# A two-layer decoder trunk: four gated heads kept on chip, two sets of transposes tied behind matmul passes, and another order at the end of the attention

## The chip, the cores and the metric

The kernel runs on one core of one Trainium2 chip. Its time is device microseconds of one execution; the figure compared is the median of several runs. Profiles are single executions taken by the hardware profiler. In them PE is TensorE's matmuls and PEld its weight loads, DVE is VectorE, ACT is ScalarE, POOL is GpSimd, and SP is the engine whose queue issues nearly all the DMAs here. Times in a trace count from the first instruction.

## The reference, cut to what matters

The model has two layers on a sequence of 512 tokens of width 1024, float32 throughout. Layer 0 mixes tokens with a gated delta rule of 16 heads, layer 1 with causal sliding-window attention, and each is followed by a gated MLP with a causal convolution of width 3:

```python
h = h + gated_deltanet(rmsnorm(h, a_norm_w[i]), ...)      # layer 0
k_sh, v_sh = shared_kv(h, kv_norm_w, w_kv)
h = h + sliding_window_sink_attention(rmsnorm(h, b_norm_w[j]), k_sh, v_sh, ...)  # layer 1
h = h + conv_gated_mlp(rmsnorm(h, ffn_norm_w[layer]), ...)  # after each mixer
```

Three steps of it are touched. The mixer ends with a gate and a projection: `o = rmsnorm(o, out_norm_w) * silu(z)`, then `o @ w_out`. The attention projects the normalised residual once to keys and values (`rmsnorm(h, kv_norm_w) @ w_kv`), and its own queries from `rmsnorm(h, b_norm_w)`. It ends with `o @ w_o`, where `o` gathers 16 heads' `probs @ v`, two heads to each of eight row blocks of 128.

## The kernel before, in words

Everything is kept transposed: channels on the 128 partitions, the 512 tokens along the free dimension, so that a *row* is a tile of 128 x 512. A float32 product is made of three matmuls: weights and activations are split into a high and a low part (`hi` rounded by a cast on ACT, `lo` the rest by a subtraction on DVE; `cast` for weights, `split` for rows), and `mm3` (L158) adds hi·hi (L162), hi·lo (L163) and lo·hi (L164) for each of the contraction blocks. A *pass* is eight blocks of three matmuls into one PSUM bank. The split weights stand in three pairs of buffers, `whi` and `wlo`; the PSUM banks are three of tag `d` (passes), two of `g` (transposes and small products), two of `s` and one of `p`.

**Who sets the order.** Each engine takes its instructions in order, and SP its DMAs. That order is not the program's: the framework's planner counts through the kernel with costs of its own and gives each engine, when it is free, the ready instruction of the highest priority. In the mixer the string `ORDER` lists jobs (one letter each: P, I, Q, V, C for the stages of the delta rule, z for a gate's projection, g for a gate), and `SHIFT` moves a letter's priority; g is moved forward by 40 places. `behind(later, earlier)` (L176) adds an order without a semaphore: the planner may not set `later` before `earlier`. Only the attention's main loop is written out by hand for TensorE (`manual_schedule`). Buffers of one tag are used in rotation: an instruction that fills a tile waits until all readers of that buffer's last tile are done.

**The columns.** Vectors that are needed as one value per partition (norm gains, convolution taps) are loaded as rows and turned by TensorE through a `g` bank into `const` tiles, in `columns` (L207, the transpose at L215, the copy out on DVE at L217). The last two calls turn the MLP's convolution taps, `fcw`. Near them in the program lie the gates' transposes, which are already tied behind the fifth block of query 0's pass (L350, tied at L759), the copy of the gates on ACT (L354), and the first products of keys (`key_norms`, L414), which also use `g`.

**The gated heads.** After the recurrence (`scan`, L607, four chunks for each of four groups of heads; its state row is `us`) the outputs lie in scratch memory in DRAM (`od`), as do the silu'd gates (`zd`, from `gate_proj`, L685). `gate(h)` (L692) loads both, scales the output's tokens on ACT (L700), turns it with four transposes on TensorE (L703), multiplies by gain and gate on DVE (L704) and stores the row to a third scratch, `yd` (L705). Heads 0 to 11 use the rows `ol` and `zl`, heads 12 to 15 `dt` (four buffers) and `va` (two buffers). The output projection then loads all 16 rows back from `yd` (L801), splits each into high and low, and runs the passes of `a_w_out`, three banks open at a time. Between them TensorE turns the input x into the residual (L821), also through `g`, with ACT copying out (L822).

**The attention** (L1140). A pass each for two key tiles and two value tiles; DVE scales them (L1158); keys are split by ACT and DVE (L1164 to L1167), values are turned by TensorE (L1171) and copied out by ACT (L1172) to `Vp`. Then `normed` makes the query's split activations, `xh` on ACT (L172) and `xl` on DVE (L173), and queries 0 and 1 follow, matmul by matmul (`one_by_one`: L1181, L1183, L1185). The loop over 16 units u then interleaves by hand: `scores(u)` (L1224, softmax on DVE and ACT up to L1253), `values(u - 2)` (L1276), `turn_back(u - 1)` (the transposes of the probabilities, L1260, copied to `pT` rows by ACT, L1262), and 12 or 11 matmuls from a stream of dense work, which holds queries 2 to 7 and the first five of eight contraction blocks of output tiles 0, 1 and 2. Behind the loop stand `values(14)`, the rest of the stream, `turn_back(15)`, blocks 5 and 6 of the three output tiles (18 matmuls), `values(15)`, and block 7 tile by tile, with each tile's addition to the residual (L1311) behind its last matmul. `values` of an odd unit ends a row block: ACT and DVE split it (L168, L169) into `ah` and `al`. Output tiles 3 to 7 follow under the planner.

Of the kernel before, what the change touches and what calls it, by code (L numbers as in the profile page):

```python
# [12 lines left out]
ALU = mybir.AluOpType  # L13
# [4 lines left out]
P = 128  # L18
# [3 lines left out]
KD = D // P  # L22
# [19 lines left out]
def kernel(  # L42
# [27 lines left out]
    V, S, G, PE, SP = nc.vector, nc.scalar, nc.gpsimd, nc.tensor, nc.sync  # L70
# [36 lines left out]
    def row(tag, dt=F32, n=T):  # L107
        return main.tile([P, n], dt, tag=tag, bufs=ROWS[tag], name=nm(tag))
# [67 lines left out]
    def behind(later, earlier):  # L176
        info = mybir.DependencyInfo(mybir.DependencyClass.NoSync, mybir.DependencyReason.DATA)
        tc.add_manual_dep(later.ins, earlier.ins.name, info, reason="order of issue")
# [8 lines left out]
    first = wpool.tile([P, 8, 256], F32, tag="stage", bufs=2, name=nm("stage"))  # L187
    for i in range(2):
        cs = slice(HQK * P + i * P, HQK * P + (i + 1) * P)
# [4 lines left out]
    ident = const([P, P], s="ident")  # L194
# [9 lines left out]
    S.activation(warm[:], epsc[:], AF.Sqrt)  # L204


    def columns(parts, n, s, q=SP, tag="acc"):  # L207
        st = row(tag, n=P)
        r = 0
        for ap in parts:  # L210
            k = ap.shape[0]
            q.dma_start(st[r : r + k, :], ap)
            r += k
        ps = bank("g")
        PE.transpose(ps[:, :n], st[:n, :], ident[:n, :n])  # L215
        t = const([P, n], s=s)
        V.tensor_copy(t[:], ps[:, :n])  # L217
        return t
# [23 lines left out]
    xh, xl = [], []  # L242
    for k in range(KD):
        ps = bank("g") if k % 2 else bank("s")
        for c in range(NC):
            PE.transpose(ps[:, c * P : (c + 1) * P], xs[c][:, k * P : (k + 1) * P], ident[:])
        h, l = row("xh", F32R), row("xl", F32R)
# [18 lines left out]
    st = [{} for _ in range(4)]  # L266
# [422 lines left out]
        SP.dma_start(zd[h], sz[:])  # L689


    def gate(h):  # L692
        ot, y = (row("ol"), row("zl")) if h < 12 else (row("dt"), row("va"))
        o3 = ot[:].rearrange("p (c e) -> p c e", c=NC)
        j = h % 4
        SP.dma_start(o3, od[h // 4, :, :, j * P : (j + 1) * P])
        SP.dma_start(y[:], zd[h])
        for c in range(NC):
            cs = slice(c * P, (c + 1) * P)
            S.activation(ot[:, cs], ot[:, cs], AF.Copy, scale=f_c[:, h, c : c + 1])  # L700
        pt = bank("g")
        for c in range(NC):
            PE.transpose(pt[:, c * P : (c + 1) * P], ot[:, c * P : (c + 1) * P], ident[:])  # L703
        V.scalar_tensor_tensor(y[:], pt[:], onw_c[:, 8:9], y[:], op0=ALU.mult, op1=ALU.mult)  # L704
        SP.dma_start(yd[h], y[:])  # L705

# [36 lines left out]
    for i, line in enumerate(ORDER):  # L745
        for word in line.split():
# [3 lines left out]
            with tc.high_priority(tc.cur_priority - target):  # L750
# [5 lines left out]
                else:  # L756
                    JOBS[a.upper()](i - 1, *n)

    for t in turned_gates:  # L759
        behind(t, passes[0][4])  # L760
    ctx.enter_context(tc.high_priority(tc.cur_priority - base - 1000000))


# [22 lines left out]
    def r2(role, dt=F32):  # L786
        return row(nxt(role, ROLES[role]), dt)
# [9 lines left out]
    for h2 in range(HV // 2):  # L797
        a, b = wide("G"), wide("L")
        for j in range(2):
            yr = r2("u")  # L800
            SP.dma_start(yr[:], yd[2 * h2 + j])  # L801
            split(yr[:], a[:, j, :], b[:, j, :])
            yh.append(a[:, j, :])
            yl.append(b[:, j, :])
# [61 lines left out]
    def normed(h, off):  # L866
        xh, xl = [], []
        for k in range(KD):
            a, b = r2("xh", F32R), r2("xl", F32R)
            split_scaled(h[k], norm_c[:, off + k : off + k + 1], a, b)  # L870
            xh.append(a)
            xl.append(b)
        return xh, xl
# [266 lines left out]
    def attention(h):  # L1140
        toep = rb[:]

        keys = [wide("G") for g in range(4)]
        kxh, kxl = normed(h, NKV)
        for kv in range(2):
            if kv == 1:
                st = load_stage(w_kv, 0, 8, 256 * kv)
            products = []
            for i in range(2):
                ps = bank("d")  # L1150
                mm3(ps[:], cast(st, 8, i) if kv else cast_rows(key_weights, i), KD, kxh, kxl)
                products.append(ps)

            if kv == 0:
                rs = rstd_rows(h)
            for i, ps in enumerate(products):
                f = r2("va")
                V.tensor_tensor(f[:], ps[:], rs[:], op=ALU.mult)  # L1158
                if kv == 0:
                    for j in range(2):  # L1160
                        g = 2 * i + j
                        near, far = [slice(64 * u, 64 * u + 64) for u in (j, 1 - j)]
                        src, hi = f[near, :], keys[g][near, 0, :]
                        S.copy(hi, src)  # L1164
                        S.copy(keys[g][far, 0, :], src)
                        V.tensor_tensor(keys[g][near, 1, :], src, hi.bitcast(F32), op=ALU.subtract)
                        V.tensor_tensor(keys[g][far, 1, :], src, hi.bitcast(F32), op=ALU.subtract)  # L1167
                else:
                    pt = bank("g")
                    for c in range(NC):  # L1170
                        PE.transpose(pt[:, c * P : (c + 1) * P], f[:, c * P : (c + 1) * P], ident[:])  # L1171
                    S.copy(Vp[:, :, i * P : (i + 1) * P], pt[:].rearrange("p (c e) -> p c e", c=NC))  # L1172
        qxh, qxl = normed(h, NB)
        stq = {}
# [1 line left out]
        ah, al = [], []  # L1176


        def one_by_one(ps, w, k, xh, xl, first, last):
            hi, lo = w  # L1180
            PE.matmul(ps, hi[:, k, :], xh, start=first, stop=False)  # L1181
            yield
            PE.matmul(ps, hi[:, k, :], xl, start=False, stop=False)  # L1183
            yield
            PE.matmul(ps, lo[:, k, :], xh, start=False, stop=last)  # L1185
            yield
# [68 lines left out]
        def turn_back(u):  # L1255
            for i in range(2):
                e, kb0, W = heads[u, i]
                pt = bank("g")
                for b in range(2 * W // P):
                    PE.transpose(pt[:, b * P : (b + 1) * P], e[:, b * P : (b + 1) * P], ident[:])  # L1260
                pT = r2("pT")
                S.copy(pT[:, 0 : 2 * W], pt[:, 0 : 2 * W])  # L1262
                heads[u, i] = (pT, kb0, W)

        def values(u):
            p, n0 = u // 2, 2 * (u % 2)
            g = p // 2
            if n0 == 0:
                heads[p] = bank("p")
            po = heads[p]  # L1270
            for i in range(2):
                pT, kb0, W = heads[u, i]
                nt = W // P
                for kb in range(nt):
                    for j in range(2):
                        PE.matmul(  # L1276
                            po[half[j], (n0 + i) * P : (n0 + i + 1) * P],
                            Vp[:, kb0 + kb, 64 * g : 64 * g + 64],
                            pT[:, (j * nt + kb) * P : (j * nt + kb + 1) * P],
                            start=kb == 0,  # L1280
                            stop=kb == nt - 1,
                        )
            if n0 == 0:
                return
            if p % 2 == 0:
                at[:] = [wide("G"), wide("L")]
            a, b = at[0][:, p % 2, :], at[1][:, p % 2, :]
            split(po[:], a, b)
            ah.append(a)
            al.append(b)  # L1290
# [13 lines left out]
                for k in range(begun):  # L1304
                    yield from one_by_one(ps[:], w, k, ah[k], al[k], k == 0, False)

        def late_outputs(opened, k):
            for m, (ps, w) in enumerate(opened):
                yield from one_by_one(ps[:], w, k, ah[k], al[k], False, k == KD - 1)
                if k == KD - 1:  # L1310
                    V.tensor_tensor(hT[m], hT[m], ps[:], op=ALU.add)  # L1311

        at, opened = [], []

# [5 lines left out]
        def take(stream, n):  # L1320
            for _ in range(n):
                next(stream, None)

        for p in range(2):
            for _ in query(p):
                pass

        with tc.manual_schedule(engines={mybir.EngineType.PE}):
            stream = dense()
            for u in range(16):  # L1330
                scores(u)
                if u > 1:
                    values(u - 2)
                if u > 0:
                    turn_back(u - 1)
                take(stream, 12 if u < 12 else 11)
            values(14)
            for _ in stream:
                pass
            turn_back(15)  # L1340
            for k in range(begun, KD - 1):
                for _ in late_outputs(opened, k):
                    pass
            values(15)
            for _ in late_outputs(opened, KD - 1):
                pass
        for m in range(3, KD):
            ps, w = out_tile(m)
            mm3(ps[:], w, KD, ah, al)
            V.tensor_tensor(hT[m], hT[m], ps[:], op=ALU.add)  # L1350
# [58 lines left out]
```

## Time and profile before

| what | us |
|---|---|
| three runs | 1426.91, 1426.93, 1429.56 |
| median | 1426.93 |
| the profiled execution | 1428.72 |
| its span, first to last instruction | 1426.9 |
| TensorE busy in the span | 1389.5 (97%) |
| VectorE busy | 1113.8 (78%) |
| ScalarE busy | 753.8 (53%) |

The page lists, for one execution, each engine's busy time, the costliest groups of instructions with the idle time ahead of them, and the chain of work that ended last. On that chain TensorE has 82% of the span, DVE 8%, DMA 6% and ACT 2%. A row of the timeline reads: start, duration, engine, line, operation, output <- inputs, shapes, number of instructions merged, and in brackets how long the engine was idle just before and what released it. Matmuls are pipelined, so the durations of neighbours overlap; the distance between two starts is what one costs. A row of the stretches table reads: from:to, length, then busy time and number of instructions for PE, PEld, DVE, ACT and POOL, the granted clock of TensorE (1.00 is full speed), the DMA share and GB/s.

### The profile page before, as it was taken

Reading aid. Unit: us, or ns where it says so; the run is one execution under the profiler, and the core shown is the slowest. Engines: PE = TensorE matmul, PEld = TensorE weight load, DVE = VectorE, ACT = ScalarE, POOL = GpSimd, SP = SyncE. Lnnn points to the kernel's source line nnn. Section 1 sums busy time; section 2 is a strip of 40 time slices with the busy share of each in tenths; the row PEclk is TensorE's granted clock in tenths of the full one; section 3 lists DMA queues with packets and bytes.
Section 4 is the critical chain, followed back from the end, with each engine's and each line's share of the span. In section 5 each row is a group of like instructions: output and inputs, shape, how many; then the busy total and the mean of one; then the engine's idle time right before and its main releaser. Section 6 shows DMA issues by size and latency. Waiting matters only on the chain.

```text
span 1426.9 us, 21762 instructions
## 1 busy us (share of the span) xinstructions
PE 1389.5 (97%) x8362; PEld 1165.5 (82%) x8362; DVE 1113.8 (78%) x2078; ACT 753.8 (53%) x1475; POOL 13.0 (1%) x37
## 2 busy tenths in 40 slices
PE   7999999999998999999999999999999999999997
PEld 5777878878876888888988889778788888988897
DVE  4996887969854447889878889878568888878996
ACT  7764566666546434444334446667544544344443
POOL 1000000000000000000000000000000000000000
PEclk9999999999999999999999999999999999999999
DMA  5324254264466324221443223122132322332222
GB/s 159 103 63 142 79 175 122 73 187 127 141 204 213 118 64 140 90 89 45 133 148 117 75 77 110 55 93 75 38 122 78 111 81 68 125 112 88 96 75 74
DMA packets 163131, 152.85 MB, mean 107 GB/s; under 512 B 24212, under 2 KB 150741, under 8 KB 163029
## 3 DMA queue, kind: packets, MB, share of 16 engines
q1 hardware_dynamic: 160770, 151.27, 33.0%
q8 instruction: 66, 1.08, 0.3%
q10 hardware_dynamic: 2259, 0.20, 0.1%
q14 instruction: 36, 0.29, 0.1%
HBM read 134.65 MB, written 16.80 MB: 106 GB/s over the span
## 4 chain that ended last, share of the span: by engine, by line
PE 82%; DVE 8%; DMA 6%; ACT 2%; issue 1%; DVEq 0%; SPq 0%; ACTq 0%
PE d L162 19%; PE d L163 19%; PE d L164 19%; DVE wlo L133 2%; PE s L617 1%; PE d L1030 1%; PE d L1185 1%; PE d L1028 1%; PE d L1183 1%; PE d L1181 1%; PE d L1029 1%; PE g L1260 1%; PE s L1030 1%; PE p L1276 1%; PE s L657 1%
## 5 line engine op out<-in xcount | busy, mean ns | idle before, releaser
L162 PE MATMUL d<-xh,whi 128*128 128x512 f32 x1128 | 445.1, 396 | 0.2
L163 PE MATMUL d<-xl,whi 128*128 128x512 f32 x1128 | 444.0, 395 | 0.0
L164 PE MATMUL d<-xh,wlo 128*128 128x512 f32 x1128 | 443.2, 395 | 0.7 <-DVE wlo L133 0.4
L132 ACT CAST whi<-stage 128x1024 fp32r<-128x1024 f32 (+2 forms) x234 | 227.3, 975 | 229.2 <-PE d L163 146.8
L133 DVE TENSOR_TENSOR wlo<-stage,whi 128x1024 fp32r<-128x1024 f32 (+2 forms) x234 | 263.5, 1129 | 66.7 <-ACT whi L132 66.2
L164 PEld LDWEIGHTS d<-xh,wlo 128*128 128x128 f32 x1128 | 211.6, 188 | 45.6 <-DVE wlo L133 1.1
L162 PEld LDWEIGHTS d<-xh,whi 128*128 128x128 f32 x1128 | 211.7, 188 | 44.1 <-ACT xh L172 0.5
L163 PEld LDWEIGHTS d<-xl,whi 128*128 128x128 f32 x1128 | 211.7, 188 | 42.9 <-issue 0.5
L260 DVE SCALAR_TENSOR_TENSOR acc<-d,cwc,acc 128x511 f32<-128x511 f32 (+2 forms) x96 | 70.7, 738 | 12.2 <-ACT acc L257 11.6
L911 ACT ACTIVATE dt<-dt 128x512 f32<-128x512 f32 x44 | 27.8, 632 | 80.1 <-DVE dt L894 80.1
L889 DVE TENSOR_TENSOR sz<-d,p6s 128x512 f32<-128x512 f32 x58 | 40.0, 689 | 36.9 <-PE d L164 35.0
L894 DVE SCALAR_TENSOR_TENSOR va<-sz,fcw,va 128x511 f32<-128x511 f32 (+1 forms) x58 | 43.4, 748 | 1.7 <-ACT va L892 0.9
L894 DVE SCALAR_TENSOR_TENSOR dt<-sz,fcw,dt 128x511 f32<-128x511 f32 (+1 forms) x58 | 43.4, 748 | 0.9
L546 DVE TENSOR_TENSOR sT<-sT,p6s 64x31 f32<-64x31 f32 (+15 forms) x124 | 40.8, 329 | 2.2 <-DVE p6s L540 0.3
L540 DVE TENSOR_TENSOR p6s<-sN,sT 64x31 f32<-64x31 f32 (+15 forms) x124 | 40.5, 327 | 2.4 <-DMA sN<-nd 0.4
L1249 ACT ACTIVATE dt<-dt,sm 128x256 f32<-128x256 f32 (+1 forms) x64 | 30.1, 471 | 19.2 <-DVE sm L1232 19.1
L132 ACT CAST whi<-st 128x768 fp32r<-128x768 f32 (+1 forms) x30 | 23.7, 792 | 30.1 <-PE p L1029 5.8
L889 DVE TENSOR_TENSOR zl<-d,p6s 128x512 f32<-128x512 f32 x30 | 20.7, 689 | 24.0 <-PE d L164 23.7
L665 ACT ACTIVATE rq<-o 128x128 f32<-128x128 f32 x64 | 19.0, 298 | 28.6 <-DVE o L660 16.0
L913 DVE TENSOR_TENSOR va<-dt,va 128x512 f32<-128x512 f32 x44 | 30.4, 691 | 1.2
L133 DVE TENSOR_TENSOR wlo<-st,whi 128x768 fp32r<-128x768 f32 (+1 forms) x30 | 26.9, 903 | 2.2 <-ACT whi L132 2.2
L892 ACT ACTIVATE dt<-sz,normc,fcw 128x512 f32<-128x512 f32 x29 | 23.6, 814 | 7.2 <-DVE sz L889 7.2
(770 smaller groups left out, 2866.7 us busy)
## 6 DMA issues: line engine op xcount, KB each, us to landing
stage<-in_ffn_w_up_dram SPq DMA_DIRECT2D x44, 1024.0 KB, 4.9
stage<-in_a_w_in_dram SPq DMA_DIRECT2D x23, 1024.0 KB, 5.1
stage<-in_ffn_w_down_dram SPq DMA_DIRECT2D x16, 768.0 KB, 6.1
stage<-in_a_w_out_dram SPq DMA_DIRECT2D x8, 1024.0 KB, 4.9
st<-in_ffn_w_down_dram SPq DMA_DIRECT2D x8, 768.0 KB
zd<-sz SPq DMA_DIRECT2D x16, 256.0 KB, 2.0
od<-o SPq DMA_DIRECT2D x16, 256.0 KB, 3.7
stage<-in_b_w_q_dram SPq DMA_DIRECT2D x4, 1024.0 KB
```

The costliest lines, as they stand in the source:

```text
L132: S.copy(hi[:, :kt, :m], src)
L133: V.tensor_tensor(lo[:, :kt, :m], src, hi[:, :kt, :m].bitcast(F32), op=ALU.subtract)
L162: PE.matmul(ps, hi[:, k, :m], xh[k], start=first and k == 0, stop=False)
L163: PE.matmul(ps, hi[:, k, :m], xl[k][:], start=False, stop=False)
L164: done.append(PE.matmul(ps, lo[:, k, :m], xh[k], start=False, stop=last and k == kt - 1))
L260: V.scalar_tensor_tensor(acc[:, d:], ps[:, : T - d], col, acc[:, d:], op0=ALU.mult, op1=ALU.add)
L540: V.tensor_tensor(tv, N[:, s, s + 1 : 32].unsqueeze(2).to_broadcast([64, n, m]), Tm[:, s : s + 1, 0:m].to_broadcast([64, n, m]), op=ALU.mult,)
L546: V.tensor_tensor(Tm[:, s + 1 : 32, 0:m], Tm[:, s + 1 : 32, 0:m], tv, op=ALU.subtract)
L889: V.tensor_tensor(u[:], ps[:], rs[:], op=ALU.mult)
L894: V.scalar_tensor_tensor(acc[:, d:], u[:, : T - d], tap(2 - d, t), acc[:, d:], op0=ALU.mult, op1=ALU.add)
L913: V.tensor_tensor(b[:], a[:], b[:], op=ALU.mult)
L1249: S.activation(ej, ej, AF.Exp, bias=ngm[:, i : i + 1], scale=-1.0, accum_out=den[:, i : i + 1])
```

## The change

Four edits, all to order or placement; the arithmetic stays.

- `gate`: heads 12 to 15 take the rows `va`, `va`, `us` and `p6s` for gate and result, and don't store the result to `yd`; it is kept in the dictionary `gated`. The output projection splits heads 12 to 15 straight from these rows and loads only heads 0 to 11 from `yd`.
- `columns`: the transposes of the two `fcw` calls are tied behind the last matmul of the second and of the fifth contraction block of query 1's pass.
- The eight transposes of the values are tied behind the first matmul of the fourth block of query 0's pass.
- End of the attention: block 5 of the three tiles (9 matmuls), `turn_back(15)`, `values(14)`, 5 matmuls of block 6, `values(15)`, the other 4, and then block 7 in three rounds over the tiles (hi·ah, lo·ah, hi·al) in place of tile by tile.

```diff
     def gate(h):
-        ot, y = (row("ol"), row("zl")) if h < 12 else (row("dt"), row("va"))
+        ot = row("ol" if h < 12 else "dt")
+        y = row("zl") if h < 12 else row(("va", "va", "us", "p6s")[h - 12])
...
-        SP.dma_start(yd[h], y[:])
+        if h < 12:
+            SP.dma_start(yd[h], y[:])
+        else:
+            gated[h] = y
...
     for t in turned_gates:
         behind(t, passes[0][4])
+    for i, t in enumerate(turned_columns[-2:]):
+        behind(t, passes[P][3 * i + 1])
...
-            yr = r2("u")
-            SP.dma_start(yr[:], yd[2 * h2 + j])
+            if h2 < 6:
+                yr = r2("u")
+                SP.dma_start(yr[:], yd[2 * h2 + j])
+            else:
+                yr = gated[2 * h2 + j]
             split(yr[:], a[:, j, :], b[:, j, :])
...
+        for t in turned_values:
+            behind(t, issued[3])
...
-            values(14)
             for _ in stream:
                 pass
+            rest = late_outputs(opened, range(begun, KD - 1))
+            take(rest, 9)
             turn_back(15)
-            for k in range(begun, KD - 1):
-                for _ in late_outputs(opened, k):
-                    pass
+            values(14)
+            take(rest, 5)
             values(15)
-            for _ in late_outputs(opened, KD - 1):
+            for _ in rest:
                 pass
+            for i in range(3):
+                for m, (ps, w) in enumerate(opened):
+                    PE.matmul(ps[:], w[i % 2][:, KD - 1, :], (ah, ah, al)[i][-1], start=False, stop=i == 2)
+                    if i == 2:
+                        V.tensor_tensor(hT[m], hT[m], ps[:], op=ALU.add)
```

`passes[P]` holds the third matmul (lo·hi) of each block of query 1's pass, and `issued` the first matmul of each block of the attention's queries; `turned_columns` and `turned_values` collect the transposes as they are made.

More of the change, by code (lines that the diff above doesn't have):

```diff
@@ L204 @@
     S.activation(warm[:], epsc[:], AF.Sqrt)
+    turned_columns = []
     def columns(parts, n, s, q=SP, tag="acc"):
@@ L214, in columns @@
         ps = bank("g")
-        PE.transpose(ps[:, :n], st[:n, :], ident[:n, :n])
+        turned_columns.append(PE.transpose(ps[:, :n], st[:n, :], ident[:n, :n]))
         t = const([P, n], s=s)
@@ L689, in gate_proj @@
         SP.dma_start(zd[h], sz[:])
+    gated = {}
     def gate(h):
-        ot, y = (row("ol"), row("zl")) if h < 12 else (row("dt"), row("va"))
+        ot = row("ol" if h < 12 else "dt")
+        y = row("zl") if h < 12 else row(("va", "va", "us", "p6s")[h - 12])
         o3 = ot[:].rearrange("p (c e) -> p c e", c=NC)
@@ L1144, in attention @@
         kxh, kxl = normed(h, NKV)
+        turned_values = []
         for kv in range(2):
@@ L1170, in attention @@
                     for c in range(NC):
-                        PE.transpose(pt[:, c * P : (c + 1) * P], f[:, c * P : (c + 1) * P], ident[:])
+                        cs = slice(c * P, (c + 1) * P)
+                        turned_values.append(PE.transpose(pt[:, cs], f[:, cs], ident[:]))
                     S.copy(Vp[:, :, i * P : (i + 1) * P], pt[:].rearrange("p (c e) -> p c e", c=NC))
@@ L1176, in attention @@
         ah, al = [], []
+        issued = []
         def one_by_one(ps, w, k, xh, xl, first, last):
             hi, lo = w
-            PE.matmul(ps, hi[:, k, :], xh, start=first, stop=False)
+            issued.append(PE.matmul(ps, hi[:, k, :], xh, start=first, stop=False))
             yield
@@ L1305, in early_outputs, with late_outputs @@
                     yield from one_by_one(ps[:], w, k, ah[k], al[k], k == 0, False)
[L1307 to L1311, printed above, removed]
+        def late_outputs(opened, ks):
+            for k in ks:
+                for ps, w in opened:
+                    yield from one_by_one(ps[:], w, k, ah[k], al[k], False, False)
         at, opened = [], []
```

## The prediction

> **What bounds the kernel now.** I read the page first, then who waited for whom on TensorE, then the chain of waits and the timelines of the four places that the change touches.
>
> ```profile
> PE 1389.5 (97%) x8362; PEld 1165.5 (82%) x8362; DVE 1113.8 (78%) x2078; ACT 753.8 (53%) x1475; POOL 13.0 (1%) x37
> ```
>
> TensorE is busy for 1389.5 of 1426.9 us, so at most some 37 us of its idle time can be won, and only where it is TensorE that waits. The change takes no matmul away; everything must come out of its waits:
>
> ```profile
> PE g L821 <- DVE va L704: 3.5, 1, 3.5
> PE d L1030 <- DVE wlo L133: 2.9, 5, 1.0
> PE g L1260 <- DVE dt L1253: 2.2, 1, 2.2
> PE g L215 <- DVE onwc L217: 1.7, 1, 1.7
> ```
>
> The columns are total, times and longest. The first row is aimed at by the gated heads, the fourth by the columns; smaller waits stand in the rows below. The sum is made against the profiled execution's own 1428.72 us (span 1426.9 and 1.8 outside it); that is 1.79 us above the median of the three runs (1426.91, 1426.93 and 1429.56 us), and part A will say what I make of that.
>
> **Part A, the last four gated heads.** The chain of waits, in order of time:
>
> ```profile
> 445.02 8.38 DMA yd<-va
> 453.42 2.53 DMA va<-zd
> 456.07 0.76 DVE va L704
> ```
>
> Heads 14 and 15 take the two `va` rows of heads 12 and 13. Those come free only when their stores to scratch have landed (8.38 us), then the loads of z follow (2.53 us), then the product L704, which frees the `g` bank that the transposes of x (L821) stand queued for. TensorE takes its instructions in order, so ready matmuls stand behind that transpose:
>
> ```profile
> 453.04 0.39 PE L162 MATMUL d<-nt,whi 128*128 128x512 f32 x1
> 456.97 0.63 PE L821 MATMUL g<-ident,f 128*128 128x128 f32 x4 [3.54 <-DVE va L704]
> ```
>
> The idle time is 3.54 us, and it has a second price, in the granted clock (PEclk, after the busy times) of the 2-us stretches that follow:
>
> ```profile
> 456.00:458.00 2.00, 1.03 (x6) 0.96 (x7) 1.44 (x2) 0.93 (x2) 0.00 (x0) 0.89 0.91 297
> 458.00:460.00 2.00, 2.00 (x8) 1.62 (x8) 1.10 (x3) 0.89 (x2) 0.00 (x0) 0.50 0.70 230
> 460.00:462.00 2.00, 1.91 (x11) 1.44 (x11) 0.35 (x1) 1.32 (x3) 0.00 (x0) 0.76 0.74 267
> ```
>
> At 0.89, 0.50 and 0.76 the array lost 2 x (0.11 + 0.50 + 0.24) = 1.70 us of work. Is that in every execution? The profiled one lies 1.79 us above the median run, nearly the same amount, two runs agree to 0.02 us, and the third is 2.6 us slower. I take it that the dip comes in some executions and that the median run had none. So the wait is worth 3.54 + 1.70 = 5.2 us to the profiled execution and 3.5 us to the median.
>
> [...] The rows above show one execution with the dip; none shown is one without it.
>
> The change gives each of the four heads its own row (`va`, `va`, `us`, `p6s`), splits the rows in place, and drops four stores (L705) and four loads (L801) from SP's queue; this queue no longer stands at the load of z behind the landing of those stores. What is late next: L700's scaling of the four heads on ACT.
>
> ```profile
> 442.49 4.79 ACT L700 ACTIVATE dt<-dt,fc 128x128 f32<-128x128 f32 x16 [0.57 <-DMA dt<-od]
> ```
>
> That is 1.2 us a head, done at 447.3; head 15's transposes and L704 (0.76 us, above) follow, so the banks are free by about 448.5, some 4.5 us before TensorE gets to 453.04. The four heads' splits only move forward. So the wait goes whole, and any dip with it. For the median: low end 2.3, if a wait of 1.2 us (one head's scaling) comes back because the planner now puts L821 earlier; high end 4.0, if half a microsecond, like that in which ACT waited ahead of L700 (0.57), is saved among the splits that waited for loads. I take 3.5.
>
> **Part B, the columns.** Two transposes of the conv taps stall TensorE in the pass of query 0:
>
> ```profile
> 43.22 0.39 PE L162 MATMUL d<-xh,whi 128*128 128x512 f32 x1
> 45.27 0.48 PE L215 MATMUL g<-ident,f 128*128 128x128 f32 x2 [1.66 <-DVE onwc L217]
> 45.50 0.48 PE L163 MATMUL d<-xl,whi 128*128 128x512 f32 x1
> ```
>
> They wait for a `g` bank. Both banks come free together, one by DVE's copy of `onwc`, one by ACT's copy of the gates:
>
> ```profile
> 45.05 0.17 DVE L217 COPY onwc<-g 128x17 f32<-128x17 f32 x1
> 44.95 0.42 ACT L354 COPY gt<-g 128x320 f32<-128x320 f32 x1
> ```
>
> Behind the second and fifth step of query 1's pass they are out of the way. But next in line for the same two banks is the key product, which stands four matmuls behind:
>
> ```profile
> 46.52 2.00 PE L414 MATMUL g<-kT 128*128 128x128 f32 x16
> ```
>
> Its keys are on ACT's queue ahead of the gates' copy, and its job has a higher priority than the query pass, so I expect the planner to put it where the transposes stood, and TensorE to wait there for the same banks. Then only the transposes' 0.23 us (45.27 to 45.50) moves, and comes back later. If L414 stays where it is, 1.8 us goes (45.27 - 43.22 less one matmul). On the loss side, the moved transposes meet the four key-product banks and may stand for one DVE operation in a busy queue, 0.7 us as the product of 0.76 us, so -0.9 with the 0.23. Nearest to the first case: +0.3 us.
>
> **Part C, the values.** Between the values' pass and query 0:
>
> ```profile
> 916.15 0.50 PE L1181 MATMUL d<-xh,whi 128*128 128x512 f32 x1
> 917.28 1.25 PE L1171 MATMUL g<-ident,va 128*128 128x128 f32 x8 [0.63 <-DVE va L1158]
> 918.54 0.50 PE L1183 MATMUL d<-xl,whi 128*128 128x512 f32 x1
> ```
>
> The 0.63 us is what the tie is after. But the matmul behind the transposes needs the first `xl`, and DVE gives it late:
>
> ```profile
> 917.74 2.73 DVE L173 SCALAR_TENSOR_TENSOR xl<-h,normc,xh 128x512 fp32r<-128x512 f32 x4
> ```
>
> The first of the four is out about 0.7 us after 917.74, at 918.45, and L1183 begins at 918.54. DVE's order ahead of it doesn't change. So with the transposes gone from this gap, L1183 still begins at 918.54: they were free there, and cost their own time behind the fourth step: 8 at 0.115 us (45.27 to 45.50 for two) = 0.9 us, less 0.2 us in which TensorE had to wait for the next `xl` anyhow: -0.7 us. What follows passes it on: DVE's scaling of query 1 waits for TensorE,
>
> ```profile
> 929.66 0.69 DVE L1200 SCALAR_TENSOR_TENSOR va<-d,p6s 128x512 f32<-128x512 f32 x1 [1.92 <-PE d L1185]
> ```
>
> and the first turn's 2.2 us wait (L1260, above) hangs on that softmax chain, so it moves along instead of swallowing the loss. Bounds -0.9 and 0 (all swallowed there).
>
> **Part D, the end of the attention.** Three waits go:
>
> ```profile
> 1017.35 0.44 PE L1276 MATMUL p<-acc,Vp 128*64 128x128 f32 x4 [0.70 <-DVE at L169]
> ```
>
> ```profile
> 1023.58 1.09 PE L1276 MATMUL p<-acc,Vp 128*64 128x128 f32 x16
> 1025.36 0.50 PE L1181 MATMUL d<-at,whi 128*128 128x512 f32 x1 [0.69 <-ACT at L168]
> 1026.09 0.50 PE L1183 MATMUL d<-at,whi 128*128 128x512 f32 x1 [0.22 <-DVE at L169]
> 1026.42 0.40 PE L1185 MATMUL d<-at,wlo 128*128 128x512 f32 x1
> 1026.65 0.39 PE L1181 MATMUL d<-at,whi 128*128 128x512 f32 x1
> ```
>
> Matmuls follow at 0.23 us (1026.42 to 1026.65). values(14) behind nine late matmuls and turn_back(15) waits no more: 0.70. The split of the last pair now has four late matmuls (0.9 us) ahead of the first use of `ah`, and six more (1.4 us) ahead of `al`: 0.69 and the 0.50 us by which 1026.09 is late (0.73 less 0.23) go. Together 1.9 us. The fourth pT row reuses values(14)'s, but there are five matmuls to cover the copy. Against it: the weights of output tile 0 used to come free 1.7 us before the last late matmul; now its hi half is read up to the third matmul from the end, and its bank is open as long.
>
> ```profile
> 1026.62 2.94 ACT L132 CAST whi<-stage 128x1024 fp32r<-128x1024 f32 x3 [1.31 <-PE d L1183]
> ```
>
> ```profile
> 1026.85 1.37 DVE L1311 TENSOR_TENSOR h<-h,d 128x512 f32<-128x512 f32 x2 [0.82 <-PE d L1185]
> 1028.14 1.22 DVE L133 TENSOR_TENSOR wlo<-stage,whi 128x1024 fp32r<-128x1024 f32 x1
> ```
>
> ```profile
> 1029.41 0.50 PE L164 MATMUL d<-sy,wlo 128*128 128x512 f32 x1
> ```
>
> Count from T, when the next matmul could start. ACT's cast starts 0.53 us after the matmul that frees it (1026.09, 1026.62): at T - 0.69 + 0.53 = T - 0.2, done T + 0.9. DVE's three adds run from T - 0.26 (0.43 us behind their matmul, 1026.42 to 1026.85) for 0.69 each: two are done at T + 1.1, all at T + 1.8. The lo half of tile 3's weights takes 1.22 us, so its first use comes at T + 2.4 (cast after two adds) or T + 3.0 (after three); four hi matmuls (0.9 us) run in the wait. TensorE loses 1.5 to 2.1 us; before, T was 1026.65 + 6 x 0.23 = 1028.0, and the wait to 1029.41 less four matmuls was 0.5. So D brings 1.9 - 1.6 = +0.3 or 1.9 - 1.0 = +0.9; all adds are ready before the cast, so I lean to the first: +0.5, bounds -0.2 and +1.1.
>
> **The sum.** For the profiled execution 5.2 + 0.3 - 0.7 + 0.5 = 5.3 us, 1423.4; for the median 3.5 + 0.3 - 0.7 + 0.5 = 3.6 us, 1423.3. With all low ends (2.3 - 0.9 - 0.9 - 0.2) the gain is 0.3, with all high ends (4.0 + 1.8 + 0 + 1.1) 6.9: 1426.6 and 1420.0.
>
> **Rivals.** *The dip is in every run*, the median's too, and the 1.79 us are something else: 1.7 us more, 1421.6. For it: the wait it follows is in the program's order. Against: the amounts.
> *The columns' stall goes whole* (L414 keeps its place): 1.5 us more, 1421.8. For it: L414 stands four matmuls later today. Against: that is about the time that the transposes and the copies out of both banks take.
> *The clock dips at query 0.* Part C leaves a gap of 2.2 us (916.15 to 918.54, less one matmul), with small waits for `xl` behind it; a dip like that of A costs 1.70 us: 1425.0. Against it, the stretches at and behind the 2.2 us wait of L1260, both at 1.00:
>
> ```profile
> 936.00:938.00 2.00, 0.98 (x7) 0.85 (x8) 1.98 (x11) 1.55 (x6) 0.00 (x0) 1.00 0.00 0
> 938.00:940.00 2.00, 2.00 (x11) 1.62 (x11) 0.76 (x4) 1.18 (x4) 0.00 (x0) 1.00 0.31 89
> ```
>
> [...]
> *Part A doesn't do what it says.* The planner sets the x transposes down elsewhere, and they wait about as long for a row of x or a bank: A is worth 0.3 us, the sum 0.4, time 1426.5. Against it: nothing that the rows show keeps a bank beyond 448.5.
> *SP's queue stands at the load for `us`.* Head 14's row is free only after the last scan's read of it:
>
> ```profile
> 433.75 1.16 PE L657 MATMUL s<-us,at 128*128 128x128 f32 x8 [0.34 <-ACT us L636]
> ```
>
> ```profile
> 424.98 0.32 SPq L801 DMA_DIRECT2D zl<-yd  x1
> ```
>
> SP issues in order. If the planner queues that load ahead of 424.98, the reloads of earlier heads stand till 434.9, 9.9 us, TensorE runs dry and pays the clock's 1.7 too: 11.6 - 3.6 = 8.0 us slower, 1434.9. It turns the sign from 1.9 us of standing on with the dip, 3.6 without. Against it: the planner queues a load when its row comes free in its own count, which is behind that scan.
>
> **How the numbers follow.** Forecast 0.55, dip in every run 0.13, columns 0.13, clock at query 0 0.04, A without effect 0.09, SP 0.06. About 0.2% (2.85 us) is what a measurement can tell from no change, so 1424.1 divides. Faster by more: three quarters of the forecast, the dip and the columns, 0.67; same: the other quarter, the clock and A without effect, 0.27; slower 0.06. The range 1419.8 to 1426.0 takes in the first four cases and nearly all of the bounds; it leaves out A without effect (0.09), SP (0.06) and 0.05 at the ends.
>
> **What would show it.** A: no wait of L821 for L704, clock at 1.00 there; a clock of 0.50 there proves me wrong. B: L414 waits about 1.7 us for a bank. C: L1183 waits some 2 us for `xl`, and L1171 runs behind the fourth step. D: waits at L1276 and L1181 gone, and 1.5 to 2.1 us for `wlo` ahead of tile 3. If TensorE's idle time hasn't shrunk by some 3 us, or runs lie as far apart as before, the forecast fails.

## The result, and the profile after

The changed kernel takes 1431.66 us (median of 18 runs, 1428.29 to 1433.54), the kernel before 1428.17 us (18 runs, 1426.91 to 1431.47). The ratio, worked out from all runs, is 1.0019, with a 95% interval of 1.0012 to 1.0027: 2.7 us slower, interval 1.7 to 3.9 (the two medians alone lie 3.5 us apart, within it). The forecast of 1423.3 us and its range (to 1426.0) were wrong. The profiled execution took 1432.94 us (span 1431.1). Its page has the same 8362 matmuls as before, and 3.3 us more of busy time on TensorE:

```profile
PE 1392.8 (97%) x8362; PEld 1170.6 (82%) x8362; DVE 1114.5 (78%) x2078; ACT 756.4 (53%) x1477; POOL 12.6 (1%) x37
```

TensorE's idle time has not shrunk: 38.3 us of the span (1431.1 less 1392.8), and 37.4 before.

Who waited for whom on TensorE (total, times, longest):

```profile
PE g L708 <- ACT ol L705: 2.4, 2, 2.0
PE g L1278 <- DVE dt L1271: 2.2, 1, 2.2
PE d L162 <- DVE acc L262: 2.1, 1, 2.1
PE d L1201 <- DVE xl L173: 1.9, 1, 1.9
PE g L416 <- DVE fcw L219: 1.3, 2, 0.9
```

The two waits that the change was aimed at are gone: the 3.5 us of the x transposes (L821 before, L835 now) and the 1.7 us of the columns' transposes. In their place stand four others of 0.9 to 2.1 us, at 305, 70, 920 and 49 us, beside the 2.2 us of the first turn of the probabilities (L1278 now, L1260 before), which was there before.

Part A did what the forecast said. The stretches in which TensorE stood and then ran slow are full now, at full clock (columns as in the prediction):

```profile
450.00:452.00 2.00, 2.00 (x13) 1.45 (x11) 1.60 (x2) 2.00 (x8) 0.00 (x0) 1.00 0.94 274
452.00:454.00 2.00, 2.00 (x14) 1.55 (x12) 1.14 (x3) 2.00 (x9) 0.00 (x0) 1.00 0.91 323
454.00:456.00 2.00, 1.94 (x11) 1.07 (x9) 1.41 (x3) 2.00 (x6) 0.00 (x0) 1.00 0.95 318
```

The busy time has grown mainly because TensorE ran at half clock four times inside the span's work, behind each of the four waits of about 2 us; before it did so once. The trace records the clock in steps of 3.41 us. Cut to these steps, one of the places reads:

```profile
67.84:71.25 3.41, 1.35 (x7) 0.78 (x6) 3.41 (x6) 2.77 (x5) 0.00 (x0) 1.00 0.13 21
71.25:74.67 3.42, 3.42 (x18) 3.42 (x18) 2.13 (x3) 0.50 (x1) 0.00 (x0) 0.50 0.29 77
```

TensorE worked 1.35 of 3.41 us, and the next 3.42 us ran at 0.50: 1.7 us lost. The wait ahead of it was only 2.06 us.

Part B went another way than forecast. TensorE's timeline in query 1's pass:

```profile
45.76 0.27 PE L217 MATMUL g<-ident,f 128*128 128x128 f32 x1
...
47.93 0.27 PE L217 MATMUL g<-ident,f 128*128 128x128 f32 x1
49.06 1.16 PE L416 MATMUL g<-kT 128*128 128x128 f32 x8 [0.86 <-DVE fcw L219]
50.70 1.16 PE L416 MATMUL g<-kT 128*128 128x128 f32 x8 [0.48 <-DVE fcw L219]
```

The tie holds the transposes where the change says. But the key products (L414 before, at 46.52) did not step into their place: they stand *behind* both transposes, and wait for DVE to copy each bank out.

Parts C and D, in the same timeline:

```profile
917.32 0.50 PE L1199 MATMUL d<-xh,whi 128*128 128x512 f32 x1
919.71 0.50 PE L1201 MATMUL d<-xl,whi 128*128 128x512 f32 x1 [1.89 <-DVE xl L173]
```

```profile
1030.47 0.84 PE L1369 MATMUL d<-at,whi 128*128 128x512 f32 x3
1031.99 0.50 PE L162 MATMUL d<-sy,whi 128*128 128x512 f32 x1 [0.68 <-ACT whi L132]
```

C's wait for the first `xl` is there as forecast. In D the waits at L1294 and in the late matmuls are gone, and the late wait is for the hi half of tile 3's weights, not the lo half.

### The profile page after: what moved, and what is told of

The parts are those of the page before. It is cut to its first block, busy times and chain, and to the rows that moved or that the text cites. A ratio compares the mean times of both kernels' runs of the same rounds, so it can differ in the third digit from the quotient of the medians.

```text
span 1431.1 us, 21752 instructions
## 1 busy us (share of the span) xinstructions
PE 1392.8 (97%) x8362; PEld 1170.6 (82%) x8362; DVE 1114.5 (78%) x2078; ACT 756.4 (53%) x1477; POOL 12.6 (1%) x37
## 4 chain that ended last, share of the span: by engine, by line
PE 84%; DVE 7%; DMA 5%; ACT 3%; issue 1%; SPq 0%; DVEq 0%; ACTq 0%
PE d L164 19%; PE d L162 19%; PE d L163 19%; DVE wlo L133 1%; PE d L1044 1%; PE d L1201 1%; PE s L619 1%; PE d L1199 1%; PE d L1203 1%; PE d L1042 1%; PE d L1043 1%; PE s L1044 1%; PE g L1278 1%; PE p L1294 1%; PE s L1042 1%
## 5 line engine op out<-in xcount | busy, mean ns | idle before, releaser
L163 PE MATMUL d<-xl,whi 128*128 128x512 f32 x1128 | 444.7, 395 | 0.0
L1201 PE MATMUL d<-xl,whi 128*128 128x512 f32 x64 | 26.4, 412 | 1.9 <-DVE xl L173 1.9
```

Of the source, the lines that this page charges most:

```text
L163: PE.matmul(ps, hi[:, k, :m], xl[k][:], start=False, stop=False)
```

## The experiments

Theory 1: the order edits B and C trade TensorE's waits for others of about 2 us, and such a wait can cost half a clock window more. Theory 2: A's rearranged mixer is what loses. Theory 3: clock dips come and go without regard to idle time.

**The four parts, each alone** (one chip; the kernel before 1428.74 us there, 35 runs). The edits are the four hunks of the diff.

Part A:

> Part A alone: the four last gated heads stay in rows; columns, values and the end of the attention as before. Theory 1 (the loss is made by parts B and C; A is worth what was forecast): the 3.54 us wait of the x transposes is gone and TensorE gains 3.5 us, 5.2 where the kernel before has the 1.71 us clock dip behind it; 3.5 to 5 us below the kernel before. Theory 2 (A's own re-planning takes it back: the wait of 2.0 us ahead of the product L708 at 305 us, with a clock dip of 1.7 us behind it, and some 1.5 us of later splits): that wait is there with A alone, and the time is 0 to 1.5 us below the kernel before. Theory 3 (clock dips come and go, whatever the idle time): 3.5 us below, with as many dips as before.

1425.04 us, ratio 0.9976 [0.9966, 0.9986]: 3.4 us gained. TensorE's waits keep no row of the x transposes (now L830), and the wait for `ol` is what it was before:

```profile
PE g L1269 <- DVE dt L1262: 2.2, 1, 2.2
PE g L215 <- DVE onwc L217: 1.6, 1, 1.6
PE d L162 <- ACT kT L168: 1.4, 1, 1.4
...
PE g L706 <- ACT ol L703: 0.7, 2, 0.5
```

So the 2.0 us at 305 us are not A's, and theory 2 falls. The wait for `kT` is new: it was 0.3 us before, and it stands at about 440 us, just ahead of the stretch that A fills.

Part B:

> Part B alone: only the columns' transposes tied behind query 1's pass. Theory 1: the moved transposes take the g banks ahead of the key product L416, the keys' norms come 3 to 5 us later, TensorE waits for them near 50 and 70 us (0.9, 0.5 and 2.1 us), with a 1.7 us clock dip in some executions; 2.5 to 4.5 us above the kernel before. Theory 2: the loss is A's, and B alone is worth -0.5 to +1 us, as the forecast had it (+0.3 gain). Theory 3: as theory 1 without the dip, 1 to 2.6 us above.

1433.34 us, ratio 1.0033 [1.0022, 1.0045]: 4.7 us lost, the whole of the change's loss and more. TensorE's waits from 40 to 110 us, then the one near 305 us in the timeline:

```profile
PE d L162 <- DVE acc L262: 2.1, 1, 2.1
PE g L416 <- DVE fcw L219: 1.2, 2, 0.7
PE g L447 <- DVE va L420: 0.5, 1, 0.5
```

```profile
304.38 0.33 PE L705 MATMUL g<-ident,ol 128*128 128x128 f32 x1 [2.37 <-ACT ol L702]
```

2.1 + 1.2 + 0.5 us, and some 2 us at 305, where the longest such wait was 0.4 us before, less the 1.7 us that went: about 4 us. Counted by the starts of the matmuls of the same number in the traces before and here, it is 3.1 us by 432 us, and 2.5 of them are lost between 32 and 94 us; with the other order of the mixer, the wait at 305 us delays what follows by little. This profiled execution has no dip at any of these places.

Part C:

> Part C alone: only the values' transposes behind the fourth step of query 0's pass. Theory 1: TensorE waits 1.9 us for the first xl where the transposes stood, the pass ends 0.7 us later, and the window of 3.41 us around that wait is less than half busy, so that it dips in some executions for 1.7 us: 0.7 to 2.4 us above the kernel before. [...]

1430.54 us, ratio 1.0012 [1.0001, 1.0023]: 1.7 us lost. In the clock's steps at query 0:

```profile
914.46:917.87 3.41, 1.53 (x7) 1.12 (x7) 3.41 (x6) 3.41 (x7) 0.00 (x0) 1.00 0.01 2
917.87:921.29 3.42, 3.42 (x14) 2.99 (x13) 3.42 (x6) 2.94 (x5) 0.00 (x0) 0.50 0.00 0
```

A wait of 1.88 us, and half a window lost behind it.

Part D:

> Part D alone: only the later last step of the attention. All theories: the small waits ahead of L1276 and L1181 go (1.9 us) and 1.0 to 1.6 us come back ahead of tile 3's lo weights; 0.3 to 0.9 us below the kernel before, 0.7 by the trace of the changed kernel. If the time is above the kernel before, the cover of the late weights is worse than counted.

1428.32 us, ratio 0.9997 [0.9988, 1.0007]: a gain of 0.4 us, not told apart from nothing by the runs. In the traces before and after, work that follows shifts by 0.7 us at this place (from 5.15 us late to 4.46), as expected.

The product of the four ratios is 1.0018; the whole change measured 1.0019. Each ratio has an interval of some 0.001 either way; within that the parts add up.

**Time at half clock.** Each run reports its mean granted clock, so (1 - clock) x span is its time at half clock, halved. Means over the runs, with standard errors:

```
kernel             runs   lost to the clock   time less that
before              35       4.6 +- 0.3        1424.1 +- 0.2
after               18       7.5 +- 0.5        1423.8 +- 0.2
part A alone        11       4.3 +- 0.5        1420.5 +- 0.4
part B alone        12       5.2 +- 0.5        1427.9 +- 0.3
part C alone        12       6.0 +- 0.7        1424.5 +- 0.4
part D alone        12       5.6 +- 0.4        1422.7 +- 0.5
```

Not all of it is a loss. In each of the twelve kernels' profiles the last 2.8 to 6.0 us of the span are at half clock, and TensorE's work is over by then; in the kernel before its last matmul ends at 1420.30 us:

```profile
1423.52:1426.87 3.35, 0.00 (x0) 0.00 (x0) 0.00 (x0) 0.00 (x0) 0.00 (x0) 0.50 0.47 179
```

This tail makes 1.4 to 3.0 us of the first column, 2.4 on average over the twelve profiles. So by estimate (from these averages) the kernel before loses some 2.2 us of work to the clock in a run and the changed one 5.1, and the last column lies some 2.4 us too low for every kernel; the differences between the rows stay about as they are.

At full clock the changed kernel would be 0.3 us faster; the clock takes 2.9 us more from it. The 0.3 is not told apart from nothing: the runs of after were made apart from the rest of the table, and the last column of the kernel before is 1424.1, 1424.7 and 1425.2 on the three chips of the experiments.

**B through another bank.** In the program the transposes of the taps stand ahead of the key products, and both take `g` banks. This version keeps the tie and gives the taps the one bank of tag p:

```diff
-    fcw = [columns([fconv_rows[l, 0:128, :]], 128, "fcw", tag="f") for l in range(2)]
+    fcw = [columns([fconv_rows[l, 0:128, :]], 128, "fcw", tag="f", via="p") for l in range(2)]
```

> Part B alone, but the two transposes of the convolution taps go through the bank of tag p in place of a g bank; same tie. Theory 1 (the two g banks are handed out in the program's order, so the transposes that are held back hold up the key products L416, which come after them in the program): the key products are set down at about 46 us as in the kernel before, or where the transposes stood, the keys' norms are no later, the waits at 50 and 70 us go, and the 4.6 us that B cost are gone: 0 to 1.7 us below the kernel before. Theory 2 (the loss comes from the planner's new order behind the tie, whatever the bank): still 3 to 5 us above.

1430.12 us beside 1430.08 us, ratio 1.0000 [0.9991, 1.0009]: B's loss is gone, nothing is gained. The timeline shows why it is nothing:

```profile
43.01 0.39 PE L162 MATMUL d<-xh,whi 128*128 128x512 f32 x1
45.25 3.49 PE L416 MATMUL g<-kT 128*128 128x128 f32 x16 [1.85 <-DVE onwc L219]
```

With the transposes out of their way the key products come first and wait for the same two copies. This is the case that the forecast had taken for B; whether its +0.3 is there, the interval can't tell. (They run at 3.49 instead of 2.00 us here: a half window follows this 1.85 us.) The waits near 70 and 305 us are gone too. Near 305 us the longest wait for `ol` is as short as it was before:

```profile
299.63 0.33 PE L705 MATMUL g<-ident,ol 128*128 128x128 f32 x1 [0.44 <-ACT ol L702]
```

One of 1.4 us stands at 199 us, in another place.

**C with the first `xl` earlier.** DVE scales two rows of values ahead of the queries' first `xl`. Once the transposes are moved, nothing needs those rows so early. (`scaled` collects the scaling of two key and two value rows, `lows` the queries' `xl`; the cut shows only the added tie.)

```diff
         qxh, qxl = normed(h, NB)
+        for t in scaled[2:]:
+            behind(t, lows[3])
```

> Part C alone, and the scaling of the two value rows on DVE is set behind the fourth xl of the queries. Theory 1 (C's loss is the 1.9 us in which TensorE has nothing while DVE scales values ahead of the first xl, with the clock dip that it makes): the wait falls to 0.7 us, the window around it stays more than half busy, and the time is 1.2 to 2 us below part C alone, -1 to +0.5 us to the kernel before. Theory 2 (C's loss is the transposes' own 0.9 us and the d banks, wherever xl comes): still 0.7 to 1.8 us above.

1429.47 us, ratio 0.9991 [0.9981, 1.0001]. DVE's timeline, TensorE's, and the clock's steps:

```profile
914.92 2.74 DVE L173 SCALAR_TENSOR_TENSOR xl<-h,normc,xh 128x512 fp32r<-128x512 f32 x4
917.58 1.28 DVE L1163 TENSOR_TENSOR va<-d,p6s 128x512 f32<-128x512 f32 x2
```

```profile
914.54 0.50 PE L1191 MATMUL d<-xh,whi 128*128 128x512 f32 x1
915.73 0.49 PE L1193 MATMUL d<-xl,whi 128*128 128x512 f32 x1 [0.69 <-DVE xl L173]
```

```profile
914.69:918.10 3.41, 2.72 (x11) 1.95 (x12) 3.38 (x6) 3.41 (x7) 0.00 (x0) 1.00 0.00 0
918.10:921.51 3.41, 3.41 (x19) 2.70 (x18) 3.41 (x7) 3.41 (x6) 0.00 (x0) 1.00 0.00 0
```

The wait is 0.69 instead of 1.88 us, the window 80% busy, no dip. C's loss of 1.7 us is gone. A gain of 1.3 us in their place is not shown: the interval reaches 1, and from 905 to 932 us the same matmuls take 27.05 us in this trace, 27.06 in the kernel before and 29.50 in part C alone (1.71 of its 2.44 us are the half window).

**The clock by itself.** Groups of matmuls with idle time of eight lengths between them, in a program of their own, of which one execution was profiled (the loops around it are left out):

```python
for k in range(steps):                      # 30 to 45
    PE.matmul(ps[:], w[:], r[:], start=k == 0, stop=k == steps - 1)
for _ in range(n):                          # 1 to 6 operations on cols columns
    V.scalar_tensor_tensor(r[:, :cols], ps[:, :cols], 0.001, xs[0][:, :cols], op0=ALU.mult, op1=ALU.add)
```

> A measurement of the clock by itself; it computes nothing of the reference (it copies half of x's columns' rows out as they are): 208 groups of 30 to 45 matmuls 128x512, with TensorE idle between them for eight lengths of about 0.8 to 5 us, in mixed order. Theory 1 (the clock is halved for one window of 3.41 us after a window that was less than about half busy, on a fixed grid of windows): no dip behind gaps below 1.7 us, about half of the gaps of 1.8 to 2 us dip, about 3 in 4 of those of 2.5 us, nearly all from 3.4 us. [...] If dips come and go by themselves, they stand inside busy groups as well.

All half-clock time lies on one grid of 3.413 us. Counted over the trace, 26 idle times of each length (25 at 0.65 us):

```
idle, us      0.32  0.65  1.0  1.5-1.6  1.8-1.9  2.2-2.3  3.0  4.4-4.5
with a dip       0     0    0        0       13       17   21       26
```

By windows at full clock: of 62 that were busy under 0.40, all were followed by a half-clock window; of 22 between 0.40 and 0.47, 15; of 518 above, none. In this trace the share of one window decides, not the idle time: here 1.83 us of idle lie within one window and 0.50 follows, there 3.05 us are divided between two and the clock stays at 1.00.

```profile
30.62:34.04 3.42, 1.59 (x8) 0.99 (x7) 1.67 (x3) 0.00 (x0) 1.00 0.00 0
34.04:37.45 3.41, 3.41 (x10) 2.63 (x9) 0.00 (x0) 0.00 (x0) 0.50 0.02 5
...
1952.33:1955.74 3.41, 1.94 (x9) 1.28 (x7) 1.39 (x2) 0.00 (x0) 1.00 0.00 0
1955.74:1959.16 3.42, 1.84 (x8) 1.56 (x9) 1.38 (x2) 0.00 (x0) 1.00 0.02 5
1959.16:1962.57 3.41, 3.41 (x17) 2.81 (x16) 0.00 (x0) 0.00 (x0) 1.00 0.00 0
```

Theory 3 falls: no dip inside busy groups, none behind 103 idle times up to 1.6 us.

**What a better version looks like.** A and D alone, twice (once beside the next two):

> Parts A and D together, columns and values as before. Theory 1 (the parts add up, since each has its own place): A alone gave 1425.04 us and D alone 1428.32 us against 1428.74 us, so 3.7 + 0.4 = 4.1 us below the kernel before. Theory 2 (each edit makes the planner set the mixer down anew, so that sums mean nothing): more than 2 us away from that.

> Parts A and D again, on the same chip as the version with the mended values. By the sum of the parts 0.9973, by the run before 0.9960 [0.9947, 0.9974]; about 1 us above the version with the mended values.

1424.26 us, ratio 0.9960 [0.9947, 0.9974], and 1424.43 us, 0.9969 [0.9957, 0.9981]. Then all four parts with both mends, and the same without the columns:

> All four parts of the change, with two mends: the taps' transposes through the p bank, and the values' scaling behind the fourth xl of the queries. Theory 1 (what the change lost is the key products held up behind the transposes in the rotation of the g banks, and the starved TensorE at query 0, each with its clock dips): the loss against the kernel before turns into a gain of about 5 us, the sum of the single ratios 0.9976, 1.0000, 0.9991 and 0.9997, that is 0.9964. Theory 2 (the four parts disturb one another, and no single place holds the loss): it stays within 2 us of the kernel before or above it.

> Parts A and D, and the values with the mended order; the columns as before. By the sum of the single ratios 0.9964, 5 us below the kernel before; the same as with the columns through the p bank, since that was worth nothing alone. Beside A and D alone it should gain 1.3 us, the 0.0009 of the mended values.

1424.17 us, 0.9971 [0.9960, 0.9981], and 1423.91 us, 0.9964 [0.9950, 0.9978], where the kernel before took 1429.48 us. The two mends turn the change's loss of 2.7 us into a gain of 4.1 (2.7 to 5.7). These versions are not told apart from A and D alone: the intervals overlap, and of the 1.3 us that the ratio of the mended values promised beside A and D, the medians show 0.5 (1424.43 to 1423.91), which is nothing to build on. All of them beat both kernels; about 3.5 of their 4.1 to 5.7 us are part A's.

## Why the prediction was wrong

**Part A was right in size.** 3.5 us forecast for the median, 3.4 us measured, 3.6 at full clock (1424.1 to 1420.5). There was luck in it. What TensorE waits for there changes from execution to execution: in the profiles that have the old gates, the x transposes wait for `va` 3.5 us once, 3.2 twice (parts B and D alone), 1.1 twice (the two mends) and 0.4 once (part C alone), and in most of them for a row of x besides. The matmuls from 432 to 475 us of the kernel before take 39.6 to 43.6 us in these six profiles (half windows taken off), 41.2 on average, and 37.6 to 38.6, 38.0 on average, in the six that have A: 3.2 us less. The one profile that I read happened to lie near the average (41.3). And A leaves a wait of its own, for `kT`, 0.4 to 1.8 us with A and at most 0.4 without, which the forecast didn't have.

What failed beside it was the reading of the runs: "the median run had none". By the estimate above, the kernel before loses 2.2 us of work a run to the clock, 1.3 half windows of 1.71 us, at changing places: in one profile behind the 3.54 us, in the profiles of parts A and D alone behind the columns' wait of 1.65 and 1.81 us and behind the first turn's. From three runs and one profile I had inferred a clean median and one dirty profile; the median of 18 runs lies 1.2 us higher than that of the three. The rival with the dip in every run was no better: part A alone has 4.3 us in the table's first column, hardly less than 4.6.

**Part B is the step that failed.** "I expect the planner to put it where the transposes stood", +0.3. It could not: the two `g` banks go to the transposes first and to the key products after them, as the program has it, and a transpose held back holds back what follows it in that order. 4.7 us were lost, 5.0 worse than forecast, and outside my bounds (-0.9). That the planner would keep to the tiles' order I had not weighed; L414 at 46.52, four matmuls behind L215, showed only that it was next, and I took "next in line" for "free to pass". The bank's part is shown by the version through the p bank, in which the loss and the waits at 49, 70 and 305 us are gone. By what path the late key products lead to the wait at 305 us stays open. Of the 4.7 us, the table above puts 3.8 at full clock, and the two traces show 3.1 without a dip.

**Part C's mechanism was right and its price short.** The wait of 1.9 us for `xl` and the transposes at their own cost came as said (-0.7), and 1.7 us were lost, interval 0.1 to 3.3. The rest is the clock: the rival with the dip at query 0, to which I gave 0.04, is what the profiles of the change and of part C show. My evidence against it, a 2.2 us wait with the clock at 1.00 behind it, was one throw of the dice: that window, from 935.42 us on, was busy for 0.53 of its length, just at the edge, and in nine of the twelve kernels' profiles the same wait is followed by half clock.

**Part D** brought 0.4 by the runs, not told apart from nothing, and 0.7 by the traces, for +0.5. Its three waits went, but the price was another than forecast: not 1.5 to 2.1 us for `wlo` ahead of tile 3, but 1.1 us for `whi` (0.68 and twice 0.22).

**The sum.** Forecast 3.6 us of gain, measured 2.7 us of loss. At full clock the single parts give 3.6 - 3.8 - 0.4 + 1.4 = 0.8 us of gain, the whole 0.3; each of these terms is sure to about half a microsecond. The other 2.9 us are half-clock windows, a term that my sum for the median did not have. The rivals in which A has no effect or SP's queue stands did not occur.

## What to carry to other kernels

Before you hold an instruction back, look at who comes after it in the rotation of its buffer: all of them were held back with it here, and the price was theirs (4.7 us in part B, none through the p bank). Price a wait of TensorE by the clock's windows, not by its length alone: in these two profiles the waits of 2.06 and 1.89 us, each with 1.71 us behind it, cost 7.4 us, and the one of 3.54 us that they replace 5.2 with its 1.70. And where runs lie 5 us apart, add up the granted clock of all of them, less the tail behind the last matmul, before reading one profile's dip as the exception.

## What the runs showed of the hardware

In these traces the granted clock is 1.00 or 0.50, in steps of 3.413 us on one fixed grid. In the trace of the groups of matmuls, one execution, a window at full clock in which TensorE was busy less than 0.40 was always followed by one at 0.50 (62 of 62), between 0.40 and 0.47 in 15 of 22 cases, above 0.47 in none of 518. In the profiles of the kernels, with matmuls of many shapes, windows busy 0.47 to 0.57 went either way (at the very end of the span up to 0.63). At the start of the span it was otherwise: in the kernel before, the three windows from 0.17 us on were busy 0.00, 0.00 and 0.22, and the clock stayed at 1.00 behind each. In the groups' trace idle time up to 1.6 us cost only itself (no dip behind 103); 1.8 to 2.3 us cost 1.71 us more in 30 of 52 cases, 3.0 us in 21 of 26. A window idle for 1.83 of its 3.42 us, a little over half, was enough (the rows from 30.62 us on). The kernels' profiles lie close to this edge: in part A's, a wait of 1.65 us left a window busy for 0.52, and half clock followed. Once at half clock, a window of the groups' trace busy 0.60 to 0.80 kept the next one at half too (13 of 13), above 0.80 it did not (77 of 77).
